# Four start addresses instead of one for the split gate and up weights of a two-block transformer kernel

## The chip, the cores and the metric

The kernel runs on one core of a Trainium2 chip. The metric is the device time of one execution in microseconds (us). Three runs of the kernel before took 2308.99, 2312.16 and 2316.94 us; their median, 2312.16 us, is the time before. A profile was taken of one further execution, which took 2311.62 us.

## The reference, cut to what matters

512 tokens of width 1024 pass through four layers. Layers 0 and 1 come from a first block, layers 2 and 3 from a second one. Each has a mixer (attention and the like, not touched here) and a feed-forward part, which begins with two matrix products of the same input, gate and up, with 2816 columns each:

```
def _swiglu(x, w_gate, w_up, w_down):                    # layers 0, 1
    g = jnp.einsum('bsd,df->bsf', x, w_gate)
    u = jnp.einsum('bsd,df->bsf', x, w_up)
    return jnp.einsum('bsf,fd->bsd', jax.nn.silu(g) * u, w_down)

def conv_ffn(h, w_up, cw, cb, w_down):                   # layers 2, 3
    gu = causal_dwconv(h @ w_up, cw, cb)
    g, u = jnp.split(gu, 2, axis=-1)
    return (jax.nn.gelu(g, approximate=True) * u) @ w_down
```

Everything is float32.

## The kernel before

All four layers run one after the other on the one core. A float32 operand of most products is split into a high part, rounded to the format that TensorE multiplies in one pass, and a low part, the rest. A product a·b is then three matmuls that add up in PSUM: high·high, high·low and low·high.

The gate and up products of a layer are computed in `quartered`. It goes through 11 units `u` of 256 columns of gate and 256 of up. The input and the weights of a unit are cut in halves of the contraction, of the columns and of the tokens, and a scheme of seven products of sums and differences replaces the eight of the plain rule. The closure `product` does one of the seven. It takes a pair of buffers for high and low parts, splits one weight block of 128 partitions x 1024 elements into them (`split`: ScalarE rounds it into `whi` by a CAST, L248, and VectorE writes the rest to `wlo`, L249), and issues 24 matmuls (L287): for 2 column groups and 4 blocks of the contraction, three each. In every one of them TensorE loads 128 columns of `whi` or `wlo` as its stationary operand (LDWEIGHTS, listed as PEld) and streams 256 columns of the input (`xh`, `xl`, `pr`, `pt` or `piece` in the rows) past them. So a layer has 77 products with 1848 matmuls, and the four layers have 7392. Outputs of a unit are three PSUM banks, tagged mm, sc and tp; the trace names matmuls by them.

The pair of buffers comes from `halves`:

```
def halves(self, place):
    return [self.tl(n, [P, 1152], F32R, 4)[:, place:place + 1024] for n in ("whi", "wlo")]
```

Each of the two names has four buffers of 1152 elements (4608 bytes per partition), used in turn. A buffer starts at a multiple of 512 bytes, and the parts begin `place` elements of four bytes further. `product` passes SHORT, which is 16 (64 bytes), in every layer. `early`, which runs the first four projections of the mixers of layers 1 to 3 with 256 streamed columns, passes SHORT too. All other users of `halves` pass nothing, so that their parts begin at byte 0; these matmuls stream 260 to 512 columns.

The input parts of `product` lie in other buffers, which start at multiples of 512 bytes and are read from there at multiples of 1024 bytes. The order of the instructions is that in which the code calls them; the semaphore waits follow from the buffers and PSUM banks. In layers 0 and 1 VectorE also adds some weight blocks (L530) and gates the results (`gated`); in layers 2 and 3 it runs a three-tap convolution over them (`convolved`, L576 to L590), and part of the additions is done by transfers from the GpSimd queue.

Of the kernel before, what the change touches and what calls it, by code (L numbers as in the profile page):

```python
# [30 lines left out]
PAD = 56  # L31
SHORT = 16
LAG = 1
EARLY = (1, 2)
CONV = 4
TAPS = 8
# [156 lines left out]
class Kernel:  # L193
# [112 lines left out]
    def early(self, srcs, x):  # L306
# [3 lines left out]
        for n, src in enumerate(srcs):  # L310
            ws.append(self.weights(src, [P, KD, P], place=SHORT))
            self.fm(ps[n][:, :256], ws[n], x, slice(0, 256))
            while self.later and n == EARLY[2 - len(self.later)]:
                self.behind(self.later.pop(0))
# [28 lines left out]
    def out_proj(self, act, nk, src, use, order, first=None):  # L343
# [36 lines left out]
        for t in range(NT):  # L380
# [3 lines left out]
            later.append(use(t, ps[t]))  # L384
            if t >= LAG and later[0]:
                self.behind(later.pop(0))
# [129 lines left out]
    def quartered(self, l, ops):  # L516
# [23 lines left out]
            return raw  # L540

        def product(ps, src, n, first):
            hi, lo = self.halves(SHORT)
            self.split(hi, lo, src)
            wh, wl = (x.rearrange("p (g k c) -> p g k c", g=2, k=4) for x in (hi, lo))
            xh, xl = ops[n]
            with self.tc.issue_after(self.last_mm.ins):
                for g in range(2):
                    out = ps[:, 256 * g:256 * g + 256]
                    for k in range(4):  # L550
                        a, b = wh[:, g, k], wl[:, g, k]
                        self.mm(out, a, xh[:, k], first and not g and not k, False, skip_group_check=True)
                        self.mm(out, a, xl[:, k], False, False, skip_group_check=True)
                        self.mm(out, b, xh[:, k], False, k == 3, skip_group_check=True)
# [42 lines left out]
        def q1(u):  # L597
            s = st[u]
            s["b11"] = load(u, 1, 1)
            s["a"] = self.bank("mm")  # L600
            product(s["a"], s["b11"], 0, True)
            s["b"] = self.bank("sc")
            if u < BANKS["sc"]:

                x = ops["parts"][0]
                self.mm(s["b"], x[:, 0, 0:P], x[:, 0])
            nc.scalar.activation(s["b"], s["a"], AF.Copy, scale=-1.0)  # L607

        def q2(u):
            s = st[u]  # L610
            s["b21"] = load(u, 2, 1)
            product(s["a"], s["b21"], 1, False)
            finish(2 * u, 0, s["a"])
# [19 lines left out]
        def q7(u):  # L633
            s = st[u]
            s["c"] = self.bank("tp")
            product(s["c"], s["x"], 4, True)
# [901 lines left out]
```

## Time and profile before

| | |
|---|---|
| median of 3 runs (lowest, highest) | 2312.16 us (2308.99, 2316.94) |
| profiled execution, its span | 2311.62 us, 2309.8 us |
| TensorE busy | 2252.5 us (98%), 14502 matmuls |
| VectorE busy | 1588.8 us (69%) |
| ScalarE busy | 1166.1 us (50%) |
| chain that ended last | TensorE 87%, VectorE 6%, ScalarE 2% |

The span is the time from the first instruction to the last. An engine's busy time is the sum of its instructions; matmuls overlap in the pipeline, so a duration of 276 ns doesn't mean that the next matmul starts 276 ns later. The pace of a stream of matmuls is read from starts: from a piece of the chain of work (so many matmuls in so many us), or from a window that TensorE fills without a break.

### The profile page before, as it was taken

The page shows a single profiled execution, that of the slowest core. Times are in us where ns is not written, and L with a number is a line of the kernel's source. Part 1 is how long each engine was busy: PE and PEld are TensorE (multiplying, and loading weights), DVE is VectorE, ACT ScalarE, POOL GpSimd, SP SyncE. Part 2 cuts the span into 40 slices and gives each one's busy share as a digit, 9 for nine tenths or more (in the row PEclk, how much of TensorE's full clock was granted, in tenths as well). Part 3 has the DMA queues.
Part 4 walks back from the last instruction along what each step waited for, and adds up shares of the span by engine and source line. Part 5 has one row for each costly group of instructions (what it writes and reads, how often), then busy time and mean ns, then how long its engine had stood idle before and what let it go on. Part 6 is the DMA issues. An engine that isn't in the chain of part 4 may idle for free.

```text
span 2309.8 us, 36807 instructions
## 1 busy us (share of the span) xinstructions
PE 2252.5 (98%) x14502; PEld 1946.8 (84%) x14502; DVE 1588.8 (69%) x2758; ACT 1166.1 (50%) x2079; POOL 114.8 (5%) x138
## 2 busy tenths in 40 slices
PE   9999999999999999999999998999999998999998
PEld 8667999988977789998888477999888847999987
DVE  5675988635455588874368668999446865899943
ACT  4574655533354555553243556677333365676632
POOL 1001000001000010000010011000000001100000
PEclk9999999999999999999999999999999999999999
DMA  6124644431333255444323328675432324877430
GB/s 201 53 79 122 197 148 139 146 118 39 113 112 93 63 156 173 138 147 128 119 66 112 86 82 229 166 203 154 123 101 75 119 65 129 212 194 184 139 110 37
DMA packets 91854, 292.63 MB, mean 127 GB/s; under 512 B 12696, under 2 KB 15640, under 8 KB 91680
## 3 DMA queue, kind: packets, MB, share of 16 engines
q1 hardware_dynamic: 84192, 263.01, 35.8%
q0 software_dynamic: 7488, 27.27, 7.2%
q8 instruction: 114, 1.87, 0.3%
q14 instruction: 60, 0.49, 0.1%
HBM read 275.43 MB, written 10.50 MB: 124 GB/s over the span
## 4 chain that ended last, share of the span: by engine, by line
PE 87%; DVE 6%; ACT 2%; DMA 2%; issue 2%; POOL 1%; DVEq 0%; POOLq 0%; SPq 0%; ACTq 0%
PE sc L287 29%; PE mm L287 28%; PE tp L287 18%; PE o L287 8%; PE tp L770 2%; DMA x<-in_up 1%; DVE wlo L249 1%; ACT whi L248 1%; DVE pr L1428 1%; DVE pr L739 0%; DVE xl L249 0%; ACT rt L406 0%; ACT rt L1386 0%; POOL pst L416 0%; DVE q L586 0%
## 5 line engine op out<-in xcount | busy, mean ns | idle before, releaser
L249 DVE TENSOR_TENSOR wlo<-wraw,whi 128x1024 fp32r<-128x1024 f32 (+5 forms) x325 | 377.5, 1163 | 418.8 <-ACT whi L248 412.4
L248 ACT CAST whi<-wraw 128x1024 fp32r<-128x1024 f32 (+4 forms) x323 | 323.9, 1005 | 584.6 <-PE sc L287 366.1
L287 PE MATMUL mm<-xh,whi 128*128 128x256 f32 (+1 forms) x1040 | 321.8, 310 | 9.9 <-ACT sc L607 9.9
L287 PE MATMUL mm<-xh,wlo 128*128 128x256 f32 (+1 forms) x1040 | 320.7, 309 | 0.0
L287 PE MATMUL mm<-xl,whi 128*128 128x256 f32 (+1 forms) x1040 | 319.2, 307 | 1.0 <-DVE xl L249 1.0
L287 PEld LDWEIGHTS mm<-xh,whi 128*128 128x128 f32 x1040 | 197.4, 190 | 26.1 <-ACT sc L607 12.1
L287 PEld LDWEIGHTS mm<-xh,wlo 128*128 128x128 f32 x1040 | 197.1, 190 | 12.4 <-issue 2.6
L287 PEld LDWEIGHTS mm<-xl,whi 128*128 128x128 f32 x1040 | 197.6, 190 | 11.2 <-DVE xl L249 1.4
L248 ACT CAST whi<-x 128x1024 fp32r<-128x1024 f32 x140 | 147.0, 1051 | 116.9 <-PE mm L287 51.3
L287 PE MATMUL sc<-pr,whi 128*128 128x256 f32 x704 | 195.8, 278 | 0.0
L287 PE MATMUL sc<-pr,wlo 128*128 128x256 f32 x704 | 195.5, 278 | 0.0
L249 DVE TENSOR_TENSOR wlo<-x,whi 128x1024 fp32r<-128x1024 f32 x140 | 171.1, 1224 | 32.0 <-ACT whi L248 31.2
L287 PEld LDWEIGHTS sc<-pr,whi 128*128 128x128 f32 x704 | 132.6, 188 | 0.7 <-ACT q L648 0.6
L287 PEld LDWEIGHTS sc<-pr,wlo 128*128 128x128 f32 x704 | 132.3, 188 | 0.0
L530 DVE TENSOR_TENSOR x<-x,wraw 128x1024 f32<-128x1024 f32 x106 | 129.2, 1224 | 1.6
L287 PE MATMUL tp<-xh,whi 128*128 128x256 f32 x400 | 113.8, 285 | 11.9 <-DVE room_a L576 8.7
L755 ACT ACTIVATE pr<-pr,mx 128x512 f32<-128x512 f32 (+3 forms) x160 | 88.3, 555 | 69.8 <-DVE mx L753 69.8
L287 PE MATMUL tp<-xl,whi 128*128 128x256 f32 x400 | 112.5, 281 | 0.0
L287 PE MATMUL tp<-xh,wlo 128*128 128x256 f32 x400 | 112.4, 281 | 0.0
L287 PE MATMUL sc<-piece,whi 128*128 128x256 f32 x352 | 98.1, 279 | 0.6 <-DVE piece L249 0.6
L287 PE MATMUL sc<-xh,whi 128*128 128x256 f32 x352 | 98.1, 279 | 0.6 <-ACT kf L642 0.6
L287 PE MATMUL sc<-xl,whi 128*128 128x256 f32 x352 | 97.8, 278 | 0.0
(494 smaller groups left out, 5800.4 us busy)
## 6 DMA issues: line engine op xcount, KB each, us to landing
wraw<-in_up SPq DMA_DIRECT2D x150, 512.0 KB, 4.3
wraw<-in_down SPq DMA_DIRECT2D x88, 512.0 KB, 3.6
x<-in_up SPq DMA_DIRECT2D x52, 512.0 KB, 5.0
x<-in_up POOLq DMA_DIRECT2D x34, 512.0 KB, 6.2
wraw<-in_i_fm SPq DMA_DIRECT2D x20, 512.0 KB, 3.6
kept<-x SPq DMA_DIRECT2D x16, 512.0 KB, 2.8
x<-kept SPq DMA_DIRECT2D x16, 512.0 KB, 3.4
wraw<-in_c_fm SPq DMA_DIRECT2D x16, 512.0 KB, 3.5
```

Of the source, the lines that this page charges most:

```text
L248: nc.scalar.copy(hi, src)
L249: nc.vector.tensor_sub(lo, src, hi.bitcast(F32))
L287: self.last_mm = self.nc.tensor.matmul(out, a, b, start=start, stop=stop, **k)
L530: sub, add = nc.vector.tensor_sub, lambda o, a, b: nc.vector.tensor_tensor(o, a, b, op=ALU.add)
L755: nc.scalar.activation(prt[t], prt[t], AF.Exp, bias=mx[:, 1, t:t + 1], scale=scale, accum_out=mx[:, 2, t:t + 1])
L770: nc.tensor.transpose(ps[:, at:at + P], prt[t][:, P * kt:P * kt + P], self.ident)
L1428: nc.vector.scalar_tensor_tensor(h[:, c], v[:, c], st[:, 3:4], g[j], op0=ALU.mult, op1=ALU.mult)
```

## The change

The table PLACES is added, and `product` takes its entry for the layer `l` where it took SHORT. The high and low parts begin 32, 64, 48 and 80 elements, that is 128, 256, 192 and 320 bytes, into their buffers in layers 0, 1, 2 and 3. The buffers have 1152 elements as before, and the furthest part ends at element 1104. `early` keeps SHORT.

```
@@ -31,6 +31,7 @@
 PAD = 56
 SHORT = 16
 LAG = 1
+PLACES = (32, 64, 48, 80)
 EARLY = (1, 2)
@@ -540,7 +541,7 @@
         def product(ps, src, n, first):
-            hi, lo = self.halves(SHORT)
+            hi, lo = self.halves(PLACES[l])
             self.split(hi, lo, src)
```

The instructions, their order on each of the five engines, and what each waits for are the same row for row; only addresses within `whi` and `wlo` differ.

## Rows read from the trace of the kernel before

**Rows 1.** The page: span, busy time, and the chain by engine and line.
```profile
span 2309.8 us, 36807 instructions
PE 2252.5 (98%) x14502; PEld 1946.8 (84%) x14502; DVE 1588.8 (69%) x2758; ACT 1166.1 (50%) x2079; POOL 114.8 (5%) x138
...
PE 87%; DVE 6%; ACT 2%; DMA 2%; issue 2%; POOL 1%; DVEq 0%; POOLq 0%; SPq 0%; ACTq 0%
```

**Rows 2.** TensorE's matmuls of L287 by stretch: from and to, length, busy (count), clock.
```profile
core 0: us, PE busy (x), PEclk, DMA share, GB/s
291.20:437.80 146.60, 146.60 (x1295) 1.00 0.46 142
874.50:896.90 22.40, 22.40 (x191) 1.00 0.62 203
897.60:1044.00 146.40, 146.40 (x1294) 1.00 0.47 143
1447.60:1492.20 44.60, 44.60 (x396) 1.00 0.71 178
1492.30:1613.90 121.60, 121.60 (x1034) 1.00 0.63 174
1615.90:1621.60 5.70, 5.70 (x50) 1.00 0.60 193
1993.00:2004.20 11.20, 11.20 (x96) 1.00 0.95 261
2011.00:2055.40 44.40, 44.40 (x394) 1.00 0.74 184
2055.60:2177.10 121.50, 121.50 (x1033) 1.00 0.62 169
2179.20:2184.90 5.70, 5.70 (x50) 1.00 0.61 189
```

**Rows 3.** The chain around 1492 us: start, length, PSUM bank, matmuls.
```profile
1484.15 5.44 PE sc L287 x48
1489.59 2.72 PE mm L287 x24
1492.31 2.91 PE sc L287 x24
1495.21 2.83 PE mm L287 x24
1498.04 5.65 PE tp L287 x48
```

**Rows 4.** Timeline at the same place: start, duration, engine, instruction.
```profile
1491.51 0.56 ACT L642 COPY kf<-sc 128x512 f32<-128x512 f32 x1
...
1491.92 0.28 PE L287 MATMUL mm<-xl,whi 128*128 128x256 f32 x1
1491.92 0.19 PEld L287 LDWEIGHTS mm<-xh,wlo 128*128 128x128 f32 x1
...
1492.03 0.28 PE L287 MATMUL mm<-xh,wlo 128*128 128x256 f32 x1
1492.12 0.19 PEld L287 LDWEIGHTS sc<-xh,whi 128*128 128x128 f32 x1
```

**Rows 5.** Matmuls of the whole run that stream 256 and 512 columns, by shape.
```profile
L287 PE MATMUL sc<-pr,whi 128*128 128x256 f32 x704 | 195.8, 278 | 0.0
...
L287 PE MATMUL sc<-whi,pr 128*128 128x512 f32 x288 | 92.6, 389 | 0.0
```

**Rows 6.** The same list for 1230 to 1330 us, `values` of layer 2.
```profile
L287 PE MATMUL sc<-whi,xl 128*128 128x332 f32 x16 | 5.1, 317 | 0.0
```

**Rows 7.** Durations of one form in two stretches: min/median/max ns.
```profile
L287 PE MATMUL mm<-xh,whi x29: 276/276/277, 1454.1 to 1490.8; 128*128 128x256 f32 x29
...
L287 PE MATMUL mm<-xh,whi x94: 281/281/282, 1495.1 to 1609.9; 128*128 128x256 f32 x94
```

**Rows 8.** Busy time of all engines in a stretch of layer 2.
```profile
core 0: us, PE busy (x) PEld busy (x) DVE busy (x) ACT busy (x) POOL busy (x), PEclk, DMA share, GB/s
1493.00:1560.00 67.00, 67.00 (x571) 67.00 (x571) 64.08 (x81) 46.27 (x69) 6.08 (x7) 1.00 0.74 194
```

**Rows 9.** VectorE's waits from 1493 to 1610 us: total, times, longest.
```profile
DVE wlo L249 <- ACT whi L248: 3.1, 10, 0.4
```

**Rows 10.** The splits by shape: with `whi`, `wlo`, and into pieces.
```profile
L248 ACT CAST whi<-wraw 128x1024 fp32r<-128x1024 f32 x279 | 292.3, 1051 | 478.7 <-PE sc L287 314.8 <-issue 68.2 <-PE mm L287 52.3
L249 DVE TENSOR_TENSOR wlo<-wraw,whi 128x1024 fp32r<-128x1024 f32 x279 | 340.7, 1223 | 367.1 <-ACT whi L248 366.1
L249 DVE TENSOR_TENSOR piece<-wraw,piece 128x1024 fp32r<-128x1024 f32 x16 | 19.5, 1219 | 8.5 <-ACT piece L248 4.3 <-PE o L287 4.2
L248 ACT CAST piece<-wraw 128x1024 fp32r<-128x1024 f32 x16 | 16.7, 1047 | 2.4 <-PE sc L287 2.4
```

More of the change, by code (lines that the diff above doesn't have):

```diff
@@ L33 @@
 LAG = 1
+PLACES = (32, 64, 48, 80)
 EARLY = (1, 2)
@@ L542, in product @@
         def product(ps, src, n, first):
-            hi, lo = self.halves(SHORT)
+            hi, lo = self.halves(PLACES[l])
             self.split(hi, lo, src)
```

## The prediction

> **What bounds the kernel now.** I read the page first: TensorE is busy for 98% of the span and has 87% of the chain that ended last [rows 1]. So a change of addresses can count in two ways. It can change the pace at which TensorE takes the 7392 matmuls of `product`, or it can change the splits that write and the loads that read the buffers, which matters only where TensorE waits for them. Then I asked for the stretches in which TensorE runs through `product` without a wait, layer by layer, with the count of matmuls and the granted clock [rows 2]. The reader is to divide length by count: 146.60 us for 1295 matmuls in layer 0 is 113.2 ns for one, 121.60 us for 1034 in layer 2 is 117.6 ns. The matmuls have the same shape and the same kind of buffers, and the clock is 1.00, the upper level of 2.4 GHz, in both. The chain says the same without the edges of a window: 5.44 us for 48 matmuls is 113.3 ns, 5.65 us is 117.7 ns [rows 3]. The durations of one form are 276 ns in the one stretch and 281 ns in the other, with a spread of one ns [rows 7]. So there are two paces, 4.4 ns apart, and nothing between.
>
> The third view is the place where the one passes into the other. Within layer 2, 396 matmuls run at the fast pace and the next 1034 at the slow one, and layer 3 does the same at 2055.5 us [rows 2]. At 1492 us a load of weights starts 0.09 us after the matmul before it, where the load before that started with its matmul, because the copy that empties its PSUM bank (L642) ends only at 1492.07 us [rows 4]; the 24 matmuls there take 2.91 us instead of 2.72, and from then on each 24 take 2.83 [rows 3]. The buffers are the same four before and after this wait. So the pace is kept from one wait to the next and is set anew when the stream restarts; at one and the same start of 64 bytes both occur.
>
> **The change part by part.** No instruction is added, removed or moved, and no wait. What is left are three terms.
>
> First, 308 splits (77 in each of four layers) write their high and low parts at another start. With the parts 64 bytes in (nearly all of the wide splits) or at byte 0, a CAST takes 1051 ns and the subtraction 1223 ns; into pieces, which begin at byte 0, they take 1047 and 1219 ns [rows 10]. The difference of 4 ns would be at most 308 x 0.004 = 1.2 us on each engine, either way, beside matmuls that keep TensorE filled. I take nothing.
>
> Second, the matmuls that now run at the slow pace. The six slow stretches have 191 + 1034 + 50 + 96 + 1033 + 50 = 2454 matmuls [rows 2]. If all went at the fast pace this would save 2454 x 4.4 ns = 10.8 us. Nothing in the trace is faster than 113.3 ns for 256 columns: a stream of 512 takes 389 ns against 276, so 256 more columns cost 113 ns [rows 5, 7], which is the fast pace itself. So 10.8 us is the end of the range below. In layers 2 and 3, 13 units' worth of it (2263 matmuls of 168 to a unit) is not all to be had. There a unit takes 168 x 117.7 ns = 19.8 us now, and VectorE is busy for 64.08 of 67.00 us, 95.6% [rows 8], or 18.9 us a unit, against 19.0 us for TensorE at the fast pace. VectorE also waits 3.1 us in 117 us for ScalarE's CAST [rows 9], 0.5 us a unit. If that wait stays, a unit takes 18.9 + 0.5 = 19.4 us, and half of the 0.75 us is given back. So all stretches fast is worth between 0.8 (layer 1) + 13.5 x 0.35 = 5.5 us and 10.8 us; I take 9.
>
> Third, the matmuls that are fast now and could become slow: 7392 - 2454 = 4938, or 21.7 us at 4.4 ns, when everything is slow. The two long stretches of layers 0 and 1, 1295 and 1294 matmuls, are 5.7 us each. A still slower pace can't be excluded from this trace, since 64 bytes is the only distance that it has with 256 columns. The nearest row at byte 0 has 332 columns: 317 ns, where 276 + 76 x 113/256 = 309.5 would be expected from the others [rows 5 to 7], 7.5 ns too long. Put on all 7392 it is 55.4 - 10.8 = 44.6 us, the end of the range above. The nearest row to an address that is a multiple of 64 bytes is `product` itself, so I keep to its two paces.
>
> The sum for the likeliest case: nothing from the splits, and as many slow stretches as chance gives. In this profile the two long stretches that follow the late copies of layers 2 and 3 are slow and those of layers 0 and 1 are fast, about a third of all matmuls. I see no reason why another start should make a restart fall differently more often than not, and expect the same third less a small lean towards the gain: 2311.6 - 2 = 2309.6 us. The profiled execution (2311.62) lies 0.5 us under the median of the runs, so the same step from the median gives 2310.2; I take 2310. The runs before differ by 8 us, which is what one or two long stretches more or fewer at 4.5 to 5.7 us would do.
>
> The Trainium skill has a rule against any effect at all: "SBUF — State Buffer", section "Who interferes with whom", gives TensorE two read ports, one for the moving operand and one for weight loads, independent of each other, and says that TensorE waits for no other engine there. By that rule the start of the weights cannot matter and the sum stays at 2312. The trace agrees in so far as it shows both paces at one address; that the slow pace exists with no wait and a full clock is not explained by it.
>
> **The rivals.** *The slow pace goes.* The distance between the weights that are loaded and the columns that stream meanwhile decides whether the two reads hinder each other, and 128 to 320 bytes are clear of it where 64 is at the edge. For it: both paces occur at 64 bytes, as at an edge, and at byte 0 matmuls of 332 columns last 7.5 ns longer than the fast pace would give [rows 6]. Against it: no address of the trace shows it, and layers 2 and 3 have little room on VectorE. Time: 2311.6 - 9 = 2302.6, from 2301 to 2306.
>
> *The slow pace spreads.* At the new starts a restart falls into the slow pace more often, and the long stretches of layers 0 and 1, which have VectorE to spare and no wait for 146 us, run slow to their end. Place: 291 and 898 us. Price: 5.7 us each, so 2311.6 + 11.4 = 2323, and up to 2333 if every stretch is slow. It decides from the point where both are slow while layers 2 and 3 stay as they are; one alone is 5.7 us and stays inside what can be told. For it: layer 0 has nothing to gain and layer 1 only 0.8 us, so a new draw can only lose there. Against it: four different starts would all have to be bad, or at least these two. A still slower pace (toward 2356) is its far end.
>
> *Addresses don't count.* Then the time is that of the median, 2312, and only the draw of the restarts moves it; this is the likeliest case with another reason.
>
> **How the numbers follow.** Pace drawn as before, with or without an effect of the addresses: 0.43. Slow pace gone in most stretches: 0.31. Slow pace spread: 0.23. A pace slower than both: 0.03. A change of 0.3%, 6.9 us, is about what can be told from none: faster means under 2305.2, slower over 2319.1. The first case falls into faster, same and slower at 0.06, 0.33 and 0.04, the second at 0.24, 0.07 and 0, the third at 0, 0.06 and 0.17, the last at 0, 0 and 0.03. Together 0.30, 0.46 and 0.24. The range of 2301 to 2325 takes in all of the second case and the third up to both long stretches and a little more; the likeliest case by itself goes from 2304 to 2318.
>
> **What would show it.** In the profile after, the stretches of each layer divided by their counts: the draw is right if both 113.3 and 117.7 ns occur again, each held from wait to wait, and the slow share is within a fifth of a third. The gain is right if layers 2 and 3 have hardly a stretch at 117.7 ns and new short waits for L576, L642 or `wlo`. The spread is right if 146 us of layers 0 and 1 become 152. Splits at other than 1051 and 1223 ns, a clock under 1.00 within a stretch, or a third pace would make the working wrong.

## The result, and the profile after

The changed kernel is slower: 2330.44 us median of 6 runs (2324.85 to 2339.41) against 2313.88 us of the kernel before (6 runs, 2308.99 to 2319.49), a ratio of 1.0084 with a 95% interval of 1.0061 to 1.0107. The profiled execution took 2337.80 us, with a span of 2336.1 us, 26.3 us more than the one of before.

The page first, spans and busy times (compare [rows 1]):

```profile
span 2336.1 us, 36807 instructions
PE 2279.0 (98%) x14502; PEld 1972.7 (84%) x14502; DVE 1589.8 (68%) x2758; ACT 1167.1 (50%) x2079; POOL 113.9 (5%) x138
```

TensorE is busy for 26.5 us more, VectorE and ScalarE for 1.0 us more. So the time went into the matmuls. Then the stretches without a long wait, from and to, length, busy (count) and granted clock; lines of the kernel have moved by one, so L287 is now L288:

```profile
core 0: us, PE busy (x), PEclk, DMA share, GB/s
291.20:442.30 151.10, 151.10 (x1274) 1.00 0.45 133
909.50:1064.80 155.30, 155.30 (x1296) 1.00 0.45 136
1472.50:1638.50 166.00, 166.00 (x1412) 1.00 0.65 173
1996.00:2017.50 21.50, 21.28 (x188) 1.00 0.81 211
2035.60:2203.30 167.70, 167.70 (x1426) 1.00 0.64 172
```

These answer to [rows 2]. Length by count gives 118.6 ns in layer 0 (128 bytes), 119.8 in layer 1 (256 bytes), 117.6 in layer 2 (192 bytes); layer 3 (320 bytes) has a stretch at 113.2 (21.28 / 188) and one at 117.6. The clock is 1.00 in all. Before had two paces; the changed kernel has four, 113.3, 117.8, about 118.65 and 120.0 ns. The chain has them without the edges of windows, here in layers 0 and 1 (start, length, bank, matmuls; compare [rows 3]):

```profile
305.58 2.85 PE mm L288 x24
308.43 5.70 PE tp L288 x48
```
```profile
943.76 2.88 PE mm L288 x24
946.64 5.76 PE tp L288 x48
```

5.70 / 48 is 118.7 ns, 5.76 / 48 is 120.0 ns. Durations tell them apart too (min/median/max, compare [rows 7]): layer 0 has a spread that no pace of before had, layer 1 is even.

```profile
L288 PE MATMUL mm<-xh,whi x115: 279/281/286, 299.7 to 440.0; 128*128 128x256 f32 x115
```
```profile
L288 PE MATMUL mm<-xh,whi x100: 283/283/284, 937.8 to 1059.9; 128*128 128x256 f32 x100
```

Averaged over the starts of all matmuls of `product` in a layer, waits left out (gaps of over 135 ns), the paces were 113.38, 113.85, 116.02 and 116.30 ns before and are 118.65, 119.97, 117.78 and 116.89 ns. Times 1848 matmuls the differences are 9.7, 11.3, 3.3 and 1.1 us, together 25.4 of the 26.3 us of the span.

The splits are as they were ([rows 10]):

```profile
L249 ACT CAST whi<-wraw 128x1024 fp32r<-128x1024 f32 x279 | 292.6, 1052 | 493.2 <-PE sc L288 318.7 <-issue 88.1 <-PE mm L288 52.4
L250 DVE TENSOR_TENSOR wlo<-wraw,whi 128x1024 fp32r<-128x1024 f32 x279 | 340.3, 1222 | 376.2 <-ACT whi L249 375.8
```

### The profile page after: what moved, and what is told of

It reads as the page before. It is cut to its first block, busy times and chain, and to the rows that moved or that the text cites. A ratio compares the mean times of both kernels' runs of the same rounds, so it can differ in the third digit from the quotient of the medians.

```text
span 2336.1 us, 36807 instructions
## 1 busy us (share of the span) xinstructions
PE 2279.0 (98%) x14502; PEld 1972.7 (84%) x14502; DVE 1589.8 (68%) x2758; ACT 1167.1 (50%) x2079; POOL 113.9 (5%) x138
## 4 chain that ended last, share of the span: by engine, by line
PE 86%; DVE 6%; ACT 3%; DMA 2%; issue 1%; POOL 1%; SPq 0%; DVEq 0%; POOLq 0%; ACTq 0%
PE sc L288 29%; PE mm L288 28%; PE tp L288 18%; PE o L288 8%; PE tp L771 2%; DMA x<-in_up 1%; DVE wlo L250 1%; ACT whi L249 1%; DVE pr L1429 1%; DVE xl L250 0%; DVE pr L740 0%; ACT rt L407 0%; ACT rt L1387 0%; DVE q L587 0%; DVE x L531 0%
## 5 line engine op out<-in xcount | busy, mean ns | idle before, releaser
L288 PE MATMUL mm<-xh,whi 128*128 128x256 f32 (+1 forms) x1040 | 325.0, 313 | 9.7 <-ACT sc L608 9.7
L288 PE MATMUL mm<-xh,wlo 128*128 128x256 f32 (+1 forms) x1040 | 323.5, 311 | 0.0
L288 PE MATMUL mm<-xl,whi 128*128 128x256 f32 (+1 forms) x1040 | 321.9, 310 | 1.0 <-DVE xl L250 1.0
L288 PEld LDWEIGHTS mm<-xh,whi 128*128 128x128 f32 x1040 | 198.7, 191 | 26.0 <-ACT sc L608 11.9
L288 PEld LDWEIGHTS mm<-xh,wlo 128*128 128x128 f32 x1040 | 198.2, 191 | 12.5 <-issue 2.6
L288 PEld LDWEIGHTS mm<-xl,whi 128*128 128x128 f32 x1040 | 198.4, 191 | 11.1 <-DVE xl L250 1.2
L288 PE MATMUL sc<-pr,whi 128*128 128x256 f32 x704 | 198.2, 282 | 0.0
L288 PE MATMUL sc<-pr,wlo 128*128 128x256 f32 x704 | 198.0, 281 | 0.0
L288 PEld LDWEIGHTS sc<-pr,whi 128*128 128x128 f32 x704 | 133.8, 190 | 0.7 <-ACT q L649 0.6
L288 PEld LDWEIGHTS sc<-pr,wlo 128*128 128x128 f32 x704 | 133.1, 189 | 0.0
L288 PE MATMUL tp<-xh,whi 128*128 128x256 f32 x400 | 115.3, 288 | 11.2 <-DVE room_a L577 8.6
L288 PE MATMUL tp<-xh,wlo 128*128 128x256 f32 x400 | 114.0, 285 | 0.0
L288 PE MATMUL tp<-xl,whi 128*128 128x256 f32 x400 | 114.0, 285 | 0.0
L288 PE MATMUL sc<-piece,whi 128*128 128x256 f32 x352 | 99.1, 282 | 0.3 <-DVE piece L250 0.3
L288 PE MATMUL sc<-xh,whi 128*128 128x256 f32 x352 | 99.0, 281 | 0.3 <-ACT kf L643 0.3
L288 PE MATMUL sc<-xh,wlo 128*128 128x256 f32 x352 | 99.0, 281 | 0.0
```

Of the source, the lines that this page charges most:

```text
L288: self.last_mm = self.nc.tensor.matmul(out, a, b, start=start, stop=stop, **k)
```

## Experiments

**Theory.** The start of the weights decides which paces are possible, and a restart, which is where the stream goes on after a wait, falls into one of them. **Rivals:** the restart alone draws the pace and the changed kernel drew badly; the layer sets it; the neighbouring engines that write the buffers set it.

**1. The matmuls alone, by start of the weights.** A kernel without the reference's computation:

```
for n, (hi, lo, at) in enumerate(CASES):       # CASES = [(p, p, 0) for p in range(0, 128, 4)]
    for r in range(RESTARTS):                  # 4
        ...                                    # 96 matmuls in product's order: hi*xh, hi*xl, lo*xh
        nc.vector.tensor_copy(kept[:, 0:w], bank[:, 0:w])   # the next batch waits for it
```

> A kernel of its own, which computes nothing of the reference: batches of 96 matmuls of 256 columns in the order of product (high·high, high·low, low·high), with the weights 0 to 496 bytes (steps of 16) past a multiple of 512 and the streamed columns at 0; four restarts at each start, each after a wait for VectorE. Theory (the start sets the pace): 64 bytes shows 113.3 or 117.8 ns, 128 bytes about 118.6, 192 bytes 117.8, 256 bytes 120.0, 320 bytes 113.3 or 117.8, as in the four layers of the changed kernel, the same in all four restarts or switching between two values at most. Rival (the restart draws the pace, whatever the address): every start shows a mix of paces from 113.3 to 120 over its four restarts.

Two batches at 64 bytes, then one each at 128, 192, 256 and 320 bytes, the same columns as above:

```profile
201.60:212.00 10.40, 10.40 (x94) 1.00 0.01 2
213.20:224.10 10.90, 10.90 (x95) 1.00 0.00 0
392.80:403.90 11.10, 11.10 (x95) 1.00 0.01 1
586.40:597.40 11.00, 11.00 (x95) 1.00 0.00 1
777.30:788.40 11.10, 11.10 (x95) 1.00 0.01 1
970.60:981.10 10.50, 10.50 (x95) 1.00 0.01 2
```

A batch starts up over some 20 matmuls, and its edges are cut here, so the pace is better taken from the starts of the matmuls after the first 40 of a batch. In the four restarts that gives, in ns:

```
start     paces of the four restarts        start     paces of the four restarts
  0       120.0  120.0  120.0  120.0        256       120.0  120.0  120.0  120.0
 64       113.3  117.8  113.3  113.3        320       113.3  113.3  113.3  113.3
 80       118.8  118.8  118.8  118.6        336       118.8  118.7  118.8  118.8
128       118.7  118.7  118.6  118.6        384       118.7  118.7  118.7  118.8
192       117.8  117.8  117.8  117.8        448       117.8  117.8  117.8  113.3
```

The theory holds in the main: each start has its own pace or two (but for 304 bytes, with 117.8, 118.4 and one batch at 123.4), the five starts of the two kernels have the ones that their layers show, and the values in the table repeat after 256 bytes, but for the draws at 64 and 448. Of all 32 starts in steps of 16 bytes only 64, 320 and 448 reach 113.3 ns. With ScalarE idle and VectorE at 3% of the span, neighbouring engines are not needed for the effect.

**2. The same by start of the streamed columns.** `CASES = [(0, 0, p) for p in range(0, 128, 4)]`

> The same batches with the weights at byte 0 and the streamed columns 0 to 496 bytes past a multiple of 512. Theory in the form that the distance from the columns to the weights counts, modulo 512: the pace at a column start of d equals that of the other run at 512 - d, so 448 shows 113.3 or 117.8 ns, 384 about 118.6, 320 117.8, 256 120.0. Rival (the weights' own start counts): every start has the one pace that byte 0 has in the other run, within 1 ns.

All four predicted values came: 448 gives 113.3, 384 gives 118.6 to 118.7, 320 gives 117.8 and 256 gives 120.0. So the columns' start counts as the weights' does, and the rival falls. But the distance alone is not the rule at steps under 64 bytes: columns at 112 run at 113.3 ns in all four restarts, whereas weights at 144, the same distance modulo 256 bytes, run at 120.0.

**3. The starts swapped between layers.** `PLACES = (80, 48, 64, 32)`

> Layers 0 to 3 at 320, 192, 256 and 128 bytes. Theory (the start sets the pace): layer 0 goes to 113.3 or 117.8 ns, layer 1 to 117.8, layer 2 to 120.0, layer 3 to 118.6, each the value that another layer had at that start. Rival (the layer or the draw sets it): layer 0 stays near 118.6 and layer 1 at 120.0, or the four mix paces. Time by the theory about 2330 us with 4 us either way; by the rival anything from 2310 to 2340.

One run: 2332.98 us (the kernel before beside it: 2308.58). In the long stretch of each layer:

```profile
290.00:436.00 146.00, 146.00 (x1289) 1.00 0.46 142
902.00:1046.00 144.00, 144.00 (x1225) 1.00 0.44 132
1470.00:1628.00 158.00, 158.00 (x1319) 1.00 0.66 174
2029.50:2196.00 166.50, 166.50 (x1406) 1.00 0.64 171
```

Layer 0 at 320 bytes is at 113.3 ns, layer 1 at 192 bytes at 117.6, layer 2 at 256 bytes at 119.8, layer 3 at 128 bytes at 118.4 with the edges of the windows. Averaged over starts, layer 1 has 117.65 ns. The pace goes with the start, not with the layer.

Layer 1 also shows that 192 bytes has a second pace. Its first stretch without a gap, 38 matmuls, runs at 113.3 ns (3.06 us for 27 of them), the next one at 117.8. The chain in the first, then the durations of one form in both (compare [rows 7]):

```profile
840.45 3.06 PE mm L288 x27
L288 PE MATMUL mm<-xh,whi x8: 276/276/276, 841.3 to 843.7; 128*128 128x256 f32 x8
L288 PE MATMUL mm<-xh,whi x22: 280/280/280, 846.9 to 857.1; 128*128 128x256 f32 x22
```

**4. One half undone, then the other.** `PLACES = (16, 16, 48, 80)` and `PLACES = (32, 64, 16, 16)`

> Layers 0 and 1 back at 64 bytes, layers 2 and 3 at 192 and 320. Theory: the loss of layers 0 and 1 (1848 x 5.3 ns and 1848 x 6.7 ns, less 0.8, some 21 us) is gone and the time is within 6 us of the kernel before, 2308 to 2320. Rival (draw): the long stretches of layers 0 and 1 are slow as often as in the changed kernel, and the time stays near 2325 to 2335.

> Layers 0 and 1 at 128 and 256 bytes as in the changed kernel, layers 2 and 3 back at 64. Theory: layer 0 at 118.65 and layer 1 at 120.0 ns, 1848 x (5.3 + 6.7) ns = 22 us less the slow share that these layers have at 64 bytes anyway (0 to 5 us): 2326 to 2334 us, ratio 1.006 to 1.010. Rival (draw of the restarts): within 0.3% of before.

With layers 0 and 1 back at 64 bytes the time is 2313.05 us (the kernel before, measured beside it, 2308.58), ratio 1.001, interval 0.9985 to 1.0035. With layers 2 and 3 back it is 2327.38 us (before 2311.46), ratio 1.0077, interval 1.0057 to 1.0097. The long stretches of layers 0 and 1, first in the one kernel and then in the other:

```profile
291.00:437.00 146.00, 145.90 (x1288) 1.00 0.47 140
900.00:1046.00 146.00, 145.91 (x1287) 1.00 0.47 143
```
```profile
291.00:442.00 151.00, 150.93 (x1272) 1.00 0.44 134
909.00:1064.00 155.00, 155.00 (x1286) 1.00 0.45 139
```

That is 113.3 ns in both layers against 118.7 and 120.5 (120.0 by the starts). The loss is that of layers 0 and 1, which ran at 113.3 ns for most of the time and can't any more; layers 2 and 3 cost at most what the interval leaves, 0.35%.

**5. Pairs of starts.** The matmuls alone again, 256 pairs each, with 48 matmuls and three restarts: `CASES = [(h, l, 0) ...]` for whi against wlo, and `CASES = [(w, w, c) ...]` for weights against columns.

> The batches alone again (48 matmuls, three restarts), streamed columns at byte 0, and whi and wlo at starts of their own: every pair of 0 to 240 bytes in steps of 16. Theory (the two starts count by their place modulo 256 bytes): equal starts give the paces of the first such run, 64/64 113.3 or 117.8 ns and the others 116.6 to 120; unequal pairs lie between the paces of the two starts, with no pair under 113.3, and pairs with 64 under the others. Rival (the bank of whi and that of wlo hinder each other, not the columns): all pairs with the same difference have one pace.

> The batches alone with equal starts of whi and wlo, 0 to 240 bytes in steps of 16, against starts of the streamed columns of 0 to 240 bytes. Theory (the start of either counts, not the distance alone): weights at 64 and columns at 0, and weights at 0 and columns at 112, reach 113.3 ns as before, and the pairs at the same distance do not all share a pace (differences over 2 ns along a diagonal). Rival (distance modulo 256 counts): along each diagonal the pace is the same within 1 ns, apart from a second pace that a restart can draw.

For whi against wlo, only 64/64, 64/192 and 192/64 reach 113.3 ns, and some unequal pairs are slower than either equal one (112/64 121.5), so the expectation that they lie between failed, and with it the one that pairs with 64 lie under the others (64/96 gave 118 to 122); the rival's constant diagonals don't occur either. For weights against columns, the batches at 113.3 ns, by the distance of the weights ahead of the columns modulo 256 bytes, and by whether the weights start at an odd or an even multiple of 16 bytes:

```
distance   odd        even
  64       24 of 24   16 of 24
 144        0 of 24   24 of 24
 192        8 of 24    4 of 24
 112, 240   0 of 48    4 of 48
all others  0 of 264   0 of 264
```

So distance is most of the rule, and the place within 32 bytes counts too: theory and rival were each half right. Neither settles distance 192, where 12 of 48 batches were fast; weights at 192 and columns at 0 are one of these pairs, with one fast batch of three. The starts of the kernel before (64 and 0) are an even pair at distance 64, one of those that can fall either way. Weights at 80 and columns at 16 are an odd pair at the same distance, which never fell. The second batch of either pair took 5.1 us for 47 matmuls, the first and the last line here; with weights at 128 and columns at 64, the two lines between, a batch took 5.3 and the next 5.1 us. These windows take in the edges of a batch, so that they compare only with each other:

```profile
1230.10:1235.20 5.10, 5.10 (x47) 1.00 0.01 3
2521.20:2526.50 5.30, 5.30 (x47) 1.00 0.00 0
2527.50:2532.60 5.10, 5.10 (x47) 1.00 0.00 0
1552.40:1557.50 5.10, 5.10 (x47) 1.00 0.01 3
```

**6. A version from this.** Weights at 80 bytes and columns at 16, in all four layers. To make room, the buffers of `whi`, `wlo` and the pieces have 1088 elements, those of the input parts 64 elements more than they had, and the others are rounded to 64 instead of 128. The lines that set the starts, with PLACE = 20 and SHIFT = 4 elements:

```
-            hi, lo = self.halves(SHORT)
+            hi, lo = self.halves(PLACE)
...
-        ops = {n: [quarter(x[:, 1024 * n:1024 * n + 1024]) for x in flat] for n in range(4)}
+        ops = {n: [quarter(x[:, SHIFT + 1024 * n:SHIFT + 1024 * n + 1024]) for x in flat] for n in range(4)}
...
-            ops[n] = [f()[:, 0:1024].bitcast(F32R).rearrange("p (a b) -> p a b", a=4) for f in (pr, low)]
+            ops[n] = [f()[:, SHIFT:SHIFT + 1024].bitcast(F32R).rearrange("p (a b) -> p a b", a=4) for f in (pr, low)]
```

> All weights of product at 80 bytes and its streamed columns at 16 bytes past a multiple of 256 (the buffers are 64 elements apart instead of 128, to make room). Theory (the two starts together set the set of paces; this pair gave 113.3 ns in each of its three restarts in the run of pairs): every stretch of the four layers at 113.3 ns, 2454 x 4.4 = 10.8 us less than the profile of the kernel before, of which VectorE gives back up to 5 in layers 2 and 3; 2299 to 2306 us, ratio 0.995 to 0.998, and less scatter. Rival (a restart can always draw a slow pace): some long stretches at 117.8 ns, time within 0.2% of before.

It is faster than the kernel before, by 0.4%: 2302.89 us (5 runs, 2300.94 to 2305.80) against 2311.46 (15 runs, 2302.32 to 2318.01), ratio 0.9962, interval 0.9950 to 0.9975. Its five runs lie within 5 us, the fifteen of before within 16. The place in layer 2 that answers to [rows 3], with the same late bank:

```profile
1486.03 5.44 PE sc L290 x48
1491.47 2.72 PE mm L290 x24
1494.19 2.82 PE sc L290 x24
1497.01 2.72 PE mm L290 x24
1499.73 5.44 PE tp L290 x48
```

The wait costs its 0.1 us and the pace comes back to 113.3 ns, where the kernel before stayed at 117.7 to the end of the layer. Averaged over starts the layers have 113.45, 113.41, 113.42 and 113.44 ns. And in the long stretch VectorE gives nothing back:

```profile
core 0: us, PE busy (x) PEld busy (x) DVE busy (x) ACT busy (x) POOL busy (x), PEclk, DMA share, GB/s
1494.50:1611.10 116.60, 116.60 (x1031) 116.55 (x1029) 113.72 (x145) 86.72 (x129) 6.94 (x8) 1.00 0.64 180
```

1031 matmuls without a wait at 113.1 ns, with VectorE busy for 97.5%. VectorE's wait for ScalarE, 3.1 us in the kernel before [rows 9], is 1.0 us here:

```profile
DVE wlo L252 <- ACT whi L251: 1.0, 4, 0.3
```

Elsewhere not all of the gain arrives. The paces alone are worth 10.8 us, as predicted, but the profiled execution is 5.7 us shorter (spans of 2309.8 and 2304.1 us), the median 8.6. In the profiled layer 3 TensorE's waits for VectorE are longer, first before and then here:

```profile
PE tp L287 <- DVE room_a L576: 3.5, 2, 3.3
PE mm L287 <- DVE wlo L249: 0.2, 1, 0.2
```
```profile
PE tp L290 <- DVE room_a L579: 4.9, 2, 4.6
PE mm L290 <- DVE wlo L252: 0.4, 1, 0.4
```

The wait for `room_a` was 5.1 us in layer 2 of the kernel before too, so it is not shown that the faster pace makes it, nor where the rest of the difference went.

**7. Two controls in the same buffers.** `PLACE, SHIFT = 16, 0` (the old starts) and `PLACE, SHIFT = 32, 4` (columns moved, weights far).

> The same buffers, but weights at 64 bytes and columns at 0 as in the kernel before. Theory: paces of 113.3 and 117.8 ns as before, time within 0.2% of before. Rival (the gain of the other kernel comes from the buffers being closer): as fast as that kernel, and no slow stretch.

> The same buffers, columns at 16 bytes and weights at 128 (the pair that gave 118.9 ns in the run of pairs, 118.0 read the other way round). Theory: all four layers at about 118.9 ns, some 25 to 30 us over the kernel with 80 bytes. Rival (moving the columns alone brings the gain): 113.3 ns as at 80 bytes.

With the old starts the time is 2310.82 us, ratio 0.9997, interval 0.9982 to 1.0012, and layer 3 ran at 117.56 ns on average: the closer buffers bring nothing. With the weights at 128 bytes one run took 2332.62 us, and the layers ran at 118.47, 118.63, 118.19 and 118.33 ns. So columns at 16 bytes bring nothing by themselves; the pair of starts does it.

## Why the prediction was wrong

Predicted were 2310 us, with a range of 2301 to 2325; measured are 2330.44. The prediction said that a third pace would make its working wrong, and two such paces came.

- **The step that failed** is the one on the draw: "I see no reason why another start should make a restart fall differently more often than not". The start decides what a restart can fall into, and how often. At 128 and 256 bytes 113.3 ns never occurred (runs 1, 3, 4 and 5), and at 192 bytes seldom: not in layer 2 of the changed kernel, but in one stretch of 38 matmuls in run 3 and one of three batches in run 5. Layers 0 and 1, which had 113.3 ns and now start at 128 and 256 bytes, lost 5.3 and 6.1 ns a matmul.
- **The two paces as bounds** failed with it. I had a row at byte 0 that was 7.5 ns too long [rows 6] and kept to the paces of 64 bytes because `product` itself is "the nearest row". (In that row the weights are the streamed operand, from byte 1280 of `whi`, and the input is loaded; both start at a multiple of 256 bytes, so the distance is that of layer 1 now.) Measured are 118.65 and 119.97 ns. The term of the third part, 4.4 ns for what becomes slow, should have gone up to the 7.5 of that row, and a pace slower than both should have had far more than 0.03.
- **The spread as a rival** named the place (layers 0 and 1, 146 us to over 151) and the sign, but as a draw, with 5.7 us for each. What happened is 9.7 and 11.3 us, because the whole layer is held there, not only its long stretch, and at slower paces.
- **Held from wait to wait**: right in the traces of all eight kernels, where no stretch of `product` changed its pace without a wait, with an addition from run 6: at good starts a wait does not matter.
- **The splits**: right, 1052 and 1222 ns. The clock was 1.00 in all stretches, as said.
- **What VectorE gives back** (up to half of the gain in layers 2 and 3): wrong for the long stretches, which it was worked out for. At 113.3 ns it was busy for 97.5% and TensorE did not wait (run 6). I had put its wait for ScalarE on top of its work, but two thirds of that wait went when TensorE got faster; and its work, 18.9 us a unit from a window of 67 us, is 113.72 us for 1031 matmuls in run 6, 18.5 us a unit.
- **The rule of the Trainium skill** in "SBUF — State Buffer", section "Who interferes with whom", that TensorE's two read ports are independent, gave no effect. The measurement decides against this conclusion: with all other engines quiet the pace of the same matmuls goes from 113.3 to 120.0 ns by the starts of the two operands (runs 1, 2 and 5).

What stays open: that the load of the next weights and the streaming of the present columns hinder each other inside the memory fits all runs, since the pace depends on both starts and, but for the draw at a restart, on nothing else that was varied; but no run shows the reads themselves. Nor is it shown what in a restart picks between two paces, at 64 bytes or elsewhere.

## What to carry to other kernels

Where TensorE is full and matmuls are short, divide each stretch by its count before anything else: a pace that comes in steps, at a full clock and without waits, can come from the operands' addresses, as here. A scan of starts in a kernel of nothing but matmuls takes one run and should go over both operands in steps of 16 bytes, with several restarts, since one good start may have a second, slower pace. A start that was fine at one place says nothing of its neighbours.

## What the runs showed of the hardware

For 256 streamed columns of split float32, the pace of a stream of matmuls depends on where weights and columns start, with a period of 256 bytes but for the draw at a restart: 113.3 ns at best, and for most starts 116.7 to 120.0, with single batches at 123 to 125 ns in runs 1 and 5 (the first batch of a run left out). With the weights 64 bytes ahead, pairs at odd multiples of 16 bytes ran at 113.3 ns in 24 of 24 batches and pairs at even multiples in 16 of 24; 144 bytes ahead it was the other way round, 0 and 24 of 24. ScalarE's and VectorE's accesses to the same buffers kept their durations within 2 ns between the kernel before and the changed one.

Streams of 512 columns did not show it at the one pair of starts that the kernel before has for them. In its projections of `L287` both operands start at multiples of 512 bytes, where 256 columns run at 120.0 ns, and 512 columns take 227 ns each, twice 113.3:

```profile
529.44 1.59 PE sc L287 x7
531.03 1.36 PE mm L287 x6
```
